# A two-level fast matrix product: a third 7-step inner product, assembly in PSUM banks, and a group ordered by a table

## The chip, the cores and the metric

The kernel runs on one core of a Trainium2 chip. The metric is the device time in microseconds of one execution; of several runs the median is given. Beside it stands one execution taken with the hardware profiler, from which all shares, waits and durations come.

## The reference

```
B, S, D = 8, 2048, 2048            # x: B x S x D float32, w: D x D float32
cs = cumsum(x, axis=1)
diff = cs - (cs shifted by one along axis 1, zero first)
out = matmul(diff, w)              # float32
```

The difference of a running sum is x again, so what is computed is the product of a 16384 x 2048 matrix and a 2048 x 2048 matrix.

## The kernel before

**Tiles.** The rows of x are 128 tiles of 128 rows. The first four (`PLAIN`) are computed directly, in bf16, while w is loaded. The other 124 form 31 groups of four tiles: g, g+1, g+2, g+3. The text calls tile g+2 `h`, g+1 `k` (or "21 of g") and g+3 `l`. A group is a 2 x 2 block matrix: tiles g and h hold the rows of the upper half, k and l those of the lower half, and each tile splits its 2048 columns into two halves (`parts`). w is split into four blocks B11, B12, B21, B22 of 1024 x 1024.

**Seven products.** A group is computed by a scheme with seven products of blocks instead of eight: P1 = A11 B11, P2 = A12 B21, P3 = S4 B22, P4 = A22 T4, P5 = S1 T1, P6 = S2 T2, P7 = S3 T3. The S are sums of blocks of x and made for each group; the T are sums of blocks of w and made once. One product, for the rows of both g and h, is 32 matmuls of 128 x 128 by 128 x 512 if it is done whole (`steps`, L519, and `product`). The same scheme can be put inside a product: then it is seven quarter products of four matmuls (`quarter`, L538, matmuls at L546), 28 in all, and needs four small sums of half rows of x for each group (`sums_in`, L517) and sums of quarter blocks of w (class `Inner`). In the steady groups P2, P3, P4 and P5 are done in that way, P1, P6 and P7 whole: 4 x 28 + 3 x 32 = 208 matmuls. The first group (`group_plain`) does all seven whole, the second (`group` with g = PLAIN + 4) does P2, P3 and P4 by quarters; these two also make the T and the inner sums of w.

**Memory.** The inner sums of w that find no place stand in DRAM (`spill`) and are brought back in each group into one buffer, `flow` (`bring_flow`, L510); other values of that buffer are computed into it by VectorE (`less`, L514, and L850). The sums S1 lie in two tiles of their own, the other S in the place of transposed tiles that are no longer needed.

**Input.** Each tile comes as two f32 halves by DMA (`load`, L100). ScalarE takes its row sums of absolute values (`weigh`, L112), VectorE turns them into a scale (`scale_of`, L129 and L131), and GpSimd into the factor `unit` that the results are multiplied by (L132). ScalarE writes the halves as scaled f16 (`narrow`, L143), and a DMA transposes each half into the tiles that the matmuls read (`turn`, L156).

**Results.** There are eight PSUM banks of 128 x 512 f32. What a bank holds goes to one of seven result tiles c: the first part by ScalarE (`keep`, L554), every further part by VectorE (`add`, L557: c = bank x unit + c). A finished c is stored by DMA (`put`, L568). Before the change each quarter product whose value belongs to two or three results is added to each of them.

**Order.** Every engine gets its instructions in the order in which the program asks for them (`after` chains them on each engine), and all DMAs of the steady part are issued by one queue, SP's. The order inside a group is that of the Python code of `group`. Instructions on different engines wait for each other by semaphores only where they touch the same data or bank.

Of the kernel before, what the change touches and what calls it, by code (L numbers as in the profile page):

```python
# [10 lines left out]
def kernel(  # L11
# [55 lines left out]
    small = ctx.enter_context(tc.tile_pool(name="small", bufs=3))  # L67
    units = ctx.enter_context(tc.tile_pool(name="units", bufs=8))
# [25 lines left out]
    scales = {}  # L94

# [9 lines left out]
    def weigh(t, sides=range(2)):  # L105
        if t < END:
            if t not in sums_of:
                sums_of[t] = small.tile([P, 2], f32, name="m")
            for i in sides:
                after(  # L110
                    "act",
                    lambda: nc.scalar.activation(  # L112
                        waste,
                        where[t][i],
                        ABS,
                        scale=1.0 / ROW,
                        accum_out=sums_of[t][:, i : i + 1],
                    ),
                )

    def scale_of(t):
        if t < END:
            m2 = sums_of.pop(t)
            m = small.tile([P, 1], f32, name="m1")
            s = scales[t] = small.tile([P, 1], f32, name="s")
            u = unit[t] = units.tile([P, 1], f32, name="u")
            after(
                "dve",
                lambda: nc.vector.tensor_scalar(m, m2[:, :1], m2[:, 1:], TINY, ADD, MAX),  # L129
            )  # L130
            after("dve", lambda: nc.vector.reciprocal(s, m))  # L131
            after("pool", lambda: nc.gpsimd.tensor_scalar(u, m, uw, None, MUL))  # L132
# [32 lines left out]
    with ExitStack() as head:  # L165
# [235 lines left out]
        scale_of(PLAIN)  # L401
        for k in range(4, KH):
            block(B11, 0, 0, k, "dve")
# [6 lines left out]
        scale_of(PLAIN + 2)  # L410
        finish_row(1)
# [17 lines left out]
        scale_of(PLAIN + 1)  # L429
        narrow(PLAIN + 1)  # L430
# [52 lines left out]
    class Inner:  # L483
        def __init__(self, b):
            self.Q1, self.Q2 = ([spare.pop() for _ in range(4)] for _ in range(2))
# [15 lines left out]
        def third(self):  # L501
            less(self.t12, self.t22, self.t12)

# [96 lines left out]
    assert not spare  # L600

    def group_plain(g, X, Y, Z, V):
# [27 lines left out]
        scale_of(h + 1)  # L630
        narrow(h + 1)
# [25 lines left out]
        scale_of(g + 4)  # L657
        narrow(g + 4)
# [20 lines left out]
        scale_of(h + 4)  # L679
        less(T4[4:], B21[4:], T2[4:])  # L680
# [10 lines left out]
        scale_of(g + 5)  # L691
        adds(C22h, Y, vh)
# [16 lines left out]
        scale_of(h + 5)  # L709
        C21 = pair()  # L710
        keeps(C21, Y, vh)
        narrow(h + 5)
        less(in_3.Q2, in_3.t22, in_3.Q1)
        turn(h + 5)
# [5 lines left out]
    def group(g, X, Y, q, e, v, w):  # L720
        h = g + 2
        five = g > PLAIN + 4
# [41 lines left out]
        if g == PLAIN + 4:  # L764
            in_3.fourth()
            less(in_4.Q1, in_4.t12, in_4.t11)
        if g > PLAIN + 4:
            total(S1g, A21g, A22g, ADD)
            total(S3g, A11g, A21g, SUB)
            total(S2g, S1g, A11g, SUB)  # L770
# [10 lines left out]
        if g == PLAIN + 4:  # L781
            total(S1g, A21g, A22g, ADD)
        add(C11g[0], q, ug)
        if g == PLAIN + 4:
            total(S3g, A11g, A21g, SUB)
        quarter(e, s1, Q.Q1, True)
        add(C11h[1], e, uh)
        if g == PLAIN + 4:
            total(S2g, S1g, A11g, SUB)
# [10 lines left out]
        if g == PLAIN + 4:  # L800
            total(S2h, S1h, A11h, SUB)
        if g > PLAIN + 4:
            scale_of(next_g)
            narrow(next_g)
            total(S2h, S1h, A11h, SUB)
# [4 lines left out]
        if g == PLAIN + 4:  # L810
            scale_of(next_g)
            narrow(next_g)
        else:
            weigh(next_h)
        load(next_k, 1)
        total(S4g, A12g, S2g, SUB)
        go(P6g, 2)
        C12g = pair()
        keeps(C12g, X, ug)
        if g == PLAIN + 4:  # L820
            weigh(next_h)
# [8 lines left out]
        if five:  # L830
            one()
            two()
        if g > PLAIN + 4:
            scale_of(next_h)
            narrow(next_h)
            load(next_l, 1)
# [9 lines left out]
        if five:  # L846
            one()
            two()
            for k in range(4):
                after('dve', lambda: nc.vector.tensor_tensor(passed[k], in_3.Q4[k], in_3.Q2[k], ADD))  # L850
            a11, a12, a22, s1, s2, s3, s4 = A5
            b11, b12, b22, r1, r2, r3, r4 = A3
            N, R = in_5, in_3
            go(P7g)
            quarter(v, a12, N.t21, True)
            C22g, C22h = [one_c()], []
            keep(C22g[0], v, vg)
            quarter(q, a11, N.t11, True)
            one4()
            add(C22g[0], q, vg)  # L860
            add(C12g[0], q, ug)
            weigh(next_k)
            go(P7g)
            quarter(w, b11, R.t11, True)
            add(C12g[0], w, ug)
            quarter(v, b12, passed, False)
            if g == PLAIN + 8:
                in_5.fourth()
                keep_flow(1)
            else:  # L870
                bring_flow(1)
            add(C12g[0], v, ug)
            put(C12g[0], g, 2)
            turn(next_g, [1])
            go(P7g)
            quarter(e, s1, N.Q1, True)
            C22g += [one_c()]
            C22h = [None, one_c()]
            keep(C22g[1], e, vg)
            keep(C22h[1], e, vh)  # L880
            go(P7g)
            two4()
            scale_of(next_k)
            add(C22g[0], X[0], vg)
            put(C22g[0], g + 1, 2)
            narrow(next_k)
            quarter(q, s2, N.Q2, False)
            add(C22g[1], q, vg)
            add(C12g[1], q, ug)
            quarter(w, r2, R.Q2, False)  # L890
            add(C12g[1], w, ug)
            add(C22g[1], X[1], vg)
            go(P7h)
            quarter(e, r1, R.Q1, False)
            add(C12g[1], e, ug)
            add(C12h[1], e, uh)
            turn(next_k, [0])
            turn(next_h, [0])
            load(next_l, 0)
            go(P7h)  # L900
            quarter(v, s4, N.t22, True)
            add(C22g[1], v, vg)
            put(C22g[1], g + 1, 3)
            load(then, 1)
            quarter(q, s3, N.Q3, False)
            C22h[0] = one_c()
            keep(C22h[0], q, vh)
            add(C22h[1], q, vh)
            add(C12h[1], q, uh)
            go(P7h)  # L910
            quarter(e, a22, passed, True)
            bring_flow(2)
            add(C22h[0], e, vh)
            add(C12h[0], q, uh)
            weigh(next_l)
            quarter(v, r4, R.t22, False)
            add(C12g[1], v, ug)
            put(C12g[1], g, 3)
            go(P7h)
            adds(C22h, Y, vh)  # L920
            puts(C22h, h + 1, 1)
            quarter(e, b22, R.Q4, False)
            add(C12h[0], e, uh)
            quarter(w, r3, R.Q3, False)
            add(C12h[0], w, uh)
            put(C12h[0], h, 2)
            add(C12h[1], w, uh)
            put(C12h[1], h, 3)
            scale_of(next_l)
        else:  # L930
            in_3.third()
            one()
            two()
            scale_of(next_h)
            narrow(next_h)
            load(next_l, 1)
            weigh(next_k)
            seven(A3, in_3, C12g, C12h, P7g)
            turn(next_g, [1])
            turn(next_h, [0])  # L940
            load(next_l, 0)
            scale_of(next_k)
            narrow(next_k)
            in_5.first()
            product((v, w), S1g, T1, True)
            C22g = pair()
            keeps(C22g, (v, w), vg)
            adds(C12g, (v, w), ug)
            puts(C12g, g, 1)
            less(in_4.Q2, in_4.t22, in_4.Q1)  # L950
            product((q, e), S1h, T1, True)
            C22h = pair()
            keeps(C22h, (q, e), vh)
            one4()
            adds(C12h, (q, e), uh)
            puts(C12h, h, 1)
            go(P7g, 2)
            two4()
            turn(next_k, [0])
            adds(C22g, X, vg)  # L960
            puts(C22g, g + 1, 1)
            in_4.fourth()
            keep_flow(2)
            go(P7h, 4)
            adds(C22h, Y, vh)
            puts(C22h, h + 1, 1)
            weigh(next_l)
            scale_of(next_l)
            in_4.third()
            load(then, 1)  # L970
# [32 lines left out]
        if next_g < END:  # L1003
            less(passed, in_2.t21, in_2.Q2)
        turn(next_l, [1])
        if g == PLAIN + 4:
            in_5.third()
# [37 lines left out]
```

## Time and profile before

| | |
|---|---|
| median of three runs | 1485.3 us (1485.26 to 1485.86) |
| profiled execution, span from the first to the last instruction | 1484.2 us |
| median of the runs less that span | 1.1 us |
| TensorE (PE) busy | 1470.2 us, 6795 matmuls |
| VectorE (DVE) busy | 1290.2 us |
| ScalarE (ACT) busy | 914.3 us |
| share of the 16 DMA engines taken by SP's queue | 93.2% |
| granted TensorE clock, mean | 0.999 |
| one steady group | 45.10 us, 208 matmuls |

The page lists for each engine the time in which it had work; matmuls are pipelined, so a busy PE says little on its own. The chain that ended last is followed back from the last instruction, each step to what released it. In the groups, "idle before" is the time the engine had nothing to run ahead of these instructions, and behind the arrow what ended it. A name such as `b` is a PSUM bank, `c` a result tile, `F` the loaded input, `x` the transposed tiles, `inner` and `S` the sums, `W` the blocks of w and the sums made of them.

### The profile page before, as it was taken

How to read it: one execution, taken by the hardware profiler on the slowest of the kernel's cores; microseconds unless marked ns; L12 is line 12 of the kernel's file. 1: busy time of each engine (PE TensorE's matmuls, PEld its weight loads, DVE VectorE, ACT ScalarE, POOL GpSimd, SP SyncE). 2: the span in 40 equal slices, each digit the busy share in tenths (PEclk: the TensorE clock that was granted, in tenths of full speed). 3: DMA queues.
4: the chain of work that ended last, by engine and by line, in shares of the span. 5: the costliest groups of instructions: out<-in, count | busy, mean ns of one | idle time of the engine just before them, and what ended most of it. 6: DMA issues, size and time to landing. Idle time of an engine off the chain costs nothing.

```text
span 1484.2 us, 21118 instructions
## 1 busy us (share of the span) xinstructions
PE 1470.2 (99%) x6795; PEld 663.3 (45%) x6795; DVE 1290.2 (87%) x2434; ACT 914.3 (62%) x1301; POOL 69.5 (5%) x136
## 2 busy tenths in 40 slices
PE   8999999999999999999999999999999999999998
PEld 3444444444444444444444444444444444444443
DVE  7998998888888888888888888888888888888887
ACT  5887566665566665665755666655666656656542
POOL 0110000000000000000000000000000000000000
PEclk9999999999999999999999999999999999999999
DMA  9999989989989999989999998999989999898983
GB/s 359 361 234 295 258 241 267 241 261 272 255 245 262 245 266 268 252 249 250 259 268 264 245 263 238 262 276 253 247 254 250 268 266 253 257 240 260 274 205 128
DMA packets 386255, 382.59 MB, mean 258 GB/s; under 512 B 275744, under 2 KB 275744, under 8 KB 386016
## 3 DMA queue, kind: packets, MB, share of 16 engines
q1 hardware_dynamic: 385584, 379.41, 93.2%
q0 software_dynamic: 560, 1.84, 0.3%
q8 instruction: 53, 0.87, 0.2%
q14 instruction: 58, 0.48, 0.1%
HBM read 180.88 MB, written 135.27 MB: 213 GB/s over the span
## 4 chain that ended last, share of the span: by engine, by line
PE 94%; DMA 2%; DVE 2%; ACT 0%; issue 0%; SPq 0%; DVEq 0%; ACTq 0%
PE b L546 46%; PE b L527 45%; PE b L260 2%; DVE c L557 2%; DMA W<-in_w_dram 2%; DMA W<-in_x_dram 0%; DMA out_dram<-c 0%; ACT wb L244 0%; PE b L385 0%; ACT o L280 0%; ACT c L554 0%; SPq L204 0%; DVEq L1040 0%; DVEq L557 0%; SPq L238 0%
## 5 line engine op out<-in xcount | busy, mean ns | idle before, releaser
L557 DVE SCALAR_TENSOR_TENSOR c<-b,u,c 128x512 f32<-128x512 f32 x1051 | 746.4, 746 | 155.1 <-PE b L546 86.9
L527 PE MATMUL b<-W,x 128*128 128x512 f16 x3072 | 716.4, 379 | 0.0
L554 ACT ACTIVATE c<-b,u 128x512 f32<-128x512 f32 x492 | 314.9, 681 | 335.4 <-PE b L546 170.2
L527 PEld LDWEIGHTS <-x 128*128 128x128 f16 x3072 | 300.6, 98 | 362.5
L143 ACT ACTIVATE F<-F,s 128x1024 f16<-128x1024 f32 x246 | 282.3, 1147 | 111.7 <-DVE s L131 107.6
L112 ACT ACTIVATE waste<-F 128x1024 uint8<-128x1024 f32 x246 | 259.5, 1055 | 95.3 <-DMA F<-in_x_dram 91.2
L546 PEld LDWEIGHTS <-x 128*128 128x128 f16 x1560 | 152.4, 98 | 190.8 <-issue 10.5
L546 PE MATMUL b<-W,x 128*128 128x512 f16 x964 | 232.9, 379 | 1.4
L546 PE MATMUL b<-W,inner 128*128 128x512 f16 x828 | 212.5, 379 | 0.0
L546 PEld LDWEIGHTS <-inner 128*128 128x128 f16 x1068 | 104.5, 98 | 126.0
L546 PE MATMUL b<-W,S 128*128 128x512 f16 x588 | 146.2, 379 | 0.0
L132 POOL TENSOR_SCALAR u<-m,uw 128x1 f32<-128x1 f32 x124 | 64.5, 525 | 1301.1 <-DVE m L129 1293.2
L517 DVE TENSOR_TENSOR x<-x,x 128x1024 f16<-128x1024 f16 (+1 forms) x214 | 120.3, 574 | 5.8 <-PE b L527 0.7
L546 PEld LDWEIGHTS <-S 128*128 128x128 f16 x704 | 68.9, 98 | 83.1
L546 PE MATMUL b<-flow,x 128*128 128x512 f16 x356 | 91.4, 379 | 0.0
L260 PE MATMUL b<-wb,xP 128*128 128x512 bf16 x240 | 57.4, 393 | 5.1 <-ACT wb L244 3.7
L546 PE MATMUL b<-inner 128*128 128x512 f16 x240 | 61.6, 379 | 0.0
L546 PE MATMUL b<-inner,x 128*128 128x512 f16 x240 | 61.6, 379 | 0.0
L112 ACT ACTIVATION_READ_ACCUMULATOR waste<-F 128x1 f32 x246 | 46.6, 189 | 0.0
L517 DVE TENSOR_TENSOR x<-S,x 128x1024 f16<-128x1024 f16 x62 | 42.3, 683 | 3.2
L514 DVE TENSOR_TENSOR flow<-W,inner 128x512 f16<-128x512 f16 x120 | 42.6, 417 | 0.0
L517 DVE TENSOR_TENSOR S<-x,x 128x1024 f16<-128x1024 f16 x62 | 42.2, 681 | 0.0
(65 smaller groups left out, 520.8 us busy)
## 6 DMA issues: line engine op xcount, KB each, us to landing
F<-in_x_dram SPq DMA_DIRECT2D x246, 512.0 KB, 5.3
out_dram<-c SPq DMA_DIRECT2D x492, 256.0 KB, 4.1
flow<-spill SPq DMA_DIRECT2D x57, 512.0 KB, 4.5
W<-in_w_dram SPq DMA_DIRECT2D x32, 512.0 KB, 9.9
W<-in_x_dram SPq DMA_DIRECT2D x16, 256.0 KB, 7.2
x<-F SPq DMA_TRANSPOSE x246, 4.0
out_dram<-o POOLq DMA_DIRECT2D x5, 256.0 KB, 4.1
out_dram<-o SPq DMA_DIRECT2D x5, 256.0 KB, 3.5
```

The costliest lines, as they stand in the source:

```text
L112: lambda: nc.scalar.activation(waste, where[t][i], ABS, scale=1.0 / ROW, accum_out=sums_of[t][:, i : i + 1],),
L132: after("pool", lambda: nc.gpsimd.tensor_scalar(u, m, uw, None, MUL))
L143: lambda: nc.scalar.activation(narrowed(t)[:, ds(i * NH, NH)], where[t][i], COPY, scale=s),
L260: lambda: nc.tensor.matmul(ps[r][n], xP[:, r, ko, :], wb[h, ko][:, ds(n * NB, NB)], start=(ko == 0), stop=(ko == KO - 1),),
L514: after("dve", lambda: nc.vector.tensor_tensor(dst[k], p[k], q[k], SUB))
L517: after("dve", lambda: nc.vector.tensor_tensor(dst.all, p.all, q.all, op))
L527: said = nc.tensor.matmul(to[n], a[k], b[k][:, n, :], start=(first and k == 0), stop=(k == KH - 1), skip_group_check=True,)
L546: said = nc.tensor.matmul(to, a[k], b[k], start=(first and k == 0), stop=(k == 3), skip_group_check=True)
L554: after("act", lambda: nc.scalar.activation(c, p, COPY, scale=u))
L557: after("dve", lambda: nc.vector.scalar_tensor_tensor(c, p, u, c, MUL, ADD))
```

## The change

The second group is now a function of its own (`group_half`), and from the third group on, 29 groups, everything is done by a class `Group`. Its steps have names (`P1.p5` is the quarter product p5 of P1, `P1.s2` a small sum, `P1.fp4` a filling of the flow buffer, `S1.g` a sum of the group, `keep.C11g0`, `add.C12h1.e`, `load0.k`, `turn1.l` and so on), and a table `ORDER` says in what order they are asked for, with -1, 0 or +1 for the group before, this one or the next. Banks and result tiles are taken from the front of a list and put back at its end.

- **P1 by seven quarter products** too, with an `Inner` of B11 (`in_1`): 5 x 28 + 2 x 32 = 204 matmuls in a group.
- **P1 and P5 are assembled in four banks** (`by_seven`): ScalarE copies a bank into another bank (`cg`) and one into a result tile (`ct`), VectorE writes the sum of a bank and that tile into a bank (`m1`, `m2`), and further quarter products accumulate on top. P6 and P7 are accumulated onto the four banks of P1. The results are then read from the finished banks, so a steady group has 27 additions `add` where it had 36, four merges, and five copies by ScalarE.
- **Row sums over the transposes:** S1 is written in the place of A21, S3 over A11, and the four small sums of P4 into the transposed tiles of k and l. The two tiles that held S1 serve as sums of B11.
- **The flow buffer** is filled six times a group: four times by VectorE (P1.p4, P3.p2, P5.p4, P5.p5), twice by DMA (P2.p4, P4.p4).
- The small numbers of a tile (row sums, scale, unit) lie in one tile of a pool of 16, and GpSimd's `unit` is asked for in a step of its own (`unit_of`).
- The last P4 has an order of its own (`END_ORDER`).

The core of the diff:

```diff
+        def by_seven(self, P, h0, h1, g0, g1):
+            self.quarter(P, "p1", h0, True)
+            self.copy(f"{P}.cg", g0, open_banks, h0)
+            self.quarter(P, "p5", h1, True)
+            self.copy(f"{P}.ct", f"{P}t", free, h1)
+            self.quarter(P, "p6", h0, False)
+            self.merge(f"{P}.m1", g1, h0, f"{P}t", fresh=True)
+            self.quarter(P, "p2", g0, False)
+            self.quarter(P, "p7", h0, False)
+            self.merge(f"{P}.m2", h1, h0, f"{P}t", let=True)
+            self.quarter(P, "p3", g1, False)
+            self.quarter(P, "p4", h0, False)
...
+        def copy(self, name, to, pool, b):
...
+                after("act", lambda: nc.scalar.copy(c, p))
...
+        def merge(self, name, to, b, c, fresh=False, let=False):
...
+                after("dve", lambda: nc.vector.tensor_tensor(t, p, s, ADD))
...
+            for a, b in ("gk", "hl"):
+                (A11, A12), (A21, A22) = half[a], half[b]
+                self.step(f"S1.{a}", total, A21, A21, A22, ADD)
+                self.step(f"S2.{a}", total, A11, A21, A11, SUB)
+                self.step(f"S4.{a}", total, A12, A12, A11, SUB)
+                self.step(f"S3.{a}", total, A11, A22, A11, SUB)
...
+    ORDER = """
+    P2.s3+0 keep.C11g0+0 P1.p2+0 load0.g+1 P1.s3+0 keep.C21h0-1 P1.p3+0 P1.p7+0
+    P2.cv+0 S1.g+0 S2.g+0 P2.s4+0 P2.p6+0 P1.m2+0 keep.C11h1+0 add.C21h0.x-1
+    load1.g+1 P1.fp4+0 turn0.l+0 P2.p2+0 P5.p1+0 add.C11h1.e+0 add.C11g0.v+0
+    keep.C11g1+0 P6g.0+0 turn1.l+0 add.C11g1.q+0 S1.h+0 P5.s1+0 put.C12g1-1
+    put.C21h0-1 weigh0.g+1 P1.p4+0 S2.h+0 P2.p3+0 add.C11g1.e+0 P5.cg+0 P2.fp4+0
+    S4.g+0 P2.p7+0 P5.s2+0 weigh1.g+1 load0.h+1 P5.p2+0 scale.g+1 unit.g+1
+    put.C11g0+0 keep.C11h0+0 add.C11h1.q+0 load1.h+1 P6g.2+0 weigh0.h+1 P6h.1+0
+    P6g.1+0 P5.s4+0 P2.p4+0 P5.s3+0 P6g.3+0 keep.C22g0+0 P6h.0+0 P5.fp5+0 S4.h+0
+    P3.s1+0 narrow0.g+1 P5.p5+0 P5.ct+0 put.C21h1-1 put.C11h1+0 keep.C12g0+0
...
+    put.C12h1+0 P1.s1+1 P4.p5+0 keep.C21g1+0 weigh0.l+1 P1.p1+1 P1.cg+1
+    put.C21g0+0 P4.p3+0 P4.p4+0 keep.C21h1+0 add.C21g1.x+0 turn0.k+1
+    add.C21g1.q+0 put.C12h0+0 P2.p1+1 P4.p7+0 P1.s2+1 P1.p5+1 P1.s4+1 weigh1.l+1
+    P1.p6+1 add.C21h1.e+0 P2.s1+1 P1.ct+1 scale.l+1 add.C21h1.q+0 P1.m1+1
+    narrow0.l+1 narrow1.l+1 P2.s2+1 P2.p5+1
+    """
...
+    END_ORDER = """
+    P4.p1 keep.C21g0 P4.p5 keep.C21g1 P4.p6 add.C21g1.q keep.C21h1 P4.p2
+    add.C21g0.x put.C21g0 P4.p3 add.C21h1.e add.C21g1.x put.C21g1 P4.p7
+    add.C21h1.q keep.C21h0 put.C21h1 P4.p4 add.C21h0.x put.C21h0
+    """.split()
```

## The prediction

> **What bounds the kernel now.** I read the page first: busy times, then the chain that ended last.
>
> ```profile
> span 1484.2 us, 21118 instructions
> PE 1470.2 (99%) x6795; PEld 663.3 (45%) x6795; DVE 1290.2 (87%) x2434; ACT 914.3 (62%) x1301; POOL 69.5 (5%) x136
> ...
> q1 hardware_dynamic: 385584, 379.41, 93.2%
> ...
> PE 94%; DMA 2%; DVE 2%; ACT 0%; issue 0%; SPq 0%; DVEq 0%; ACTq 0%
> ```
>
> TensorE works 99% of the span and is 94% of the chain. VectorE (87%) and the DMA engines (93.2%) stand close behind. Next I cut one steady group of four row tiles out of the middle, and the end, by the view of windows (columns: stretch, its length, busy time and count of PE, PEld, DVE, ACT, POOL, granted clock, DMA share, GB/s):
>
> ```profile
> 76.14:124.50 48.36, 48.36 (x225) 21.91 (x224) 46.28 (x95) 39.45 (x56) 5.49 (x6) 1.00 1.02 262
> ...
> 667.00:712.10 45.10, 45.05 (x210) 20.34 (x209) 39.43 (x76) 28.72 (x42) 1.92 (x4) 1.00 0.93 263
> ...
> 1478.70:1484.20 5.50, 0.00 (x0) 0.00 (x0) 1.74 (x3) 0.00 (x0) 0.00 (x0) 0.71 0.38 143
> ```
>
> The first row is the plain group. A steady group takes 45.10 us, and there are 29 of them (29 x 45.10 = 1308 us). In it DVE has 5.7 us to spare. Then the chain of waits over one group boundary (start, length, what):
>
> ```profile
> 1200.09 6.06 PE b L546 x28
> 1206.14 0.03 issue
> 1206.17 0.02 DVEq L557
> 1206.19 0.04 issue
> 1206.24 0.76 DVE c L557
> 1207.00 0.04 issue
> 1207.04 1.02 PE b L546 x4
> 1208.06 6.91 PE b L527 x32
> ```
>
> Thirty-two matmuls take 6.91 us, so a step of four takes 0.864 us, and 52 steps are 44.90 us. The missing 0.20 us is the hop in these lines: a matmul step ends, an addition reads its bank, and the next use of that bank waits. The last matmul's end comes 0.17 us after the pace (a step alone is 1.03 us long), then 0.09 to DVE, 0.76, 0.04 back: 1.06 us. One step between (0.86) covers all but 0.20 of it. This hop is my measure for the new order. It is the only place in a steady group where PE waits. Last, durations by the page's groups (busy time, mean ns) and spacings by the timeline of DVE (start, length):
>
> ```profile
> L557 DVE SCALAR_TENSOR_TENSOR c<-b,u,c 128x512 f32<-128x512 f32 x1051 | 746.4, 746 | 155.1 <-PE b L546 86.9 <-ACT c L554 35.7 <-DVE c L557 0.9
> ...
> L280 ACT COPY o<-b 128x512 f32<-128x512 f32 x10 | 5.2, 599 | 0.0
> ```
>
> ```profile
> 669.11 1.42 DVE L514 TENSOR_TENSOR flow<-W,inner 128x512 f16<-128x512 f16 x4
> ...
> 701.29 6.87 DVE L557 SCALAR_TENSOR_TENSOR c<-b,u,c 128x512 f32<-128x512 f32 x10 [0.83 <-ACT c L554]
> ```
>
> Ten additions in 6.87 us: one starts every 0.68 us though each lasts 0.75. Four f16 subtractions of half a row in 1.42: one every 0.33, each 0.42 long.
>
> **The change, per steady group.** Counts are those of the built programs, divided by 29 groups.
> *Removed on PE:* A11·B11 goes from 32 to 28 matmuls: one step, 0.864 us. 51 steps are 44.04 us. Without any wait that is 45.10 - 44.04 = 1.06 us a group, 30.7 in all, of which 5.8 are the old hop, which the new order no longer has in that place.
> *DVE:* nine additions fewer (P1 and P5 are put together in PSUM and leave as four results each), -9 x 0.68 = -6.1. Four small sums more, 4 x 0.34 = +1.4 (a half-row sum starts every 0.34 too). The fills of the flow buffer go from two to four, eight half rows, 8 x 0.33 = +2.7. Four merges (bank plus f32 tile into a bank), a form without a row: at least 0.33 (the half-row f16 sum), at most 1.5 (two additions); I take 0.68, since the addition has the same bank and f32 operands and width: +2.7. Sum +0.7: 40.1 of 44.04 us, 91%; with the ends of the merge 38.7 and 43.4, below 44.04 either way. By the Trainium skill, page "VectorE: DVE Perf Modes", section on the TRN2 errata, an f32 tensor_tensor of N elements takes (N+151)/0.96 ns, 691 ns here; by that the merge would be 0.06 shorter than the addition's 0.746 and the sum the same within 0.3 us.
> *ACT:* five copies out of banks, three of them into banks (no row; nearest the 599 ns copy out of a bank, the ends being 0.3, half of it, and 0.75): +3.0, 28.7 to 31.7 of 44.04. ACT's idle time hides it; without that cover a copy in the way of PE would cost its 0.6.
> *Moved:* units (0.53 us each) stand alone on POOL, which is busy 1.9 of 45 us; nothing but the results' scaling waits for them. Loads, transposes, results and the two flow loads are the same 34 DMAs on the same SP queue, in another order. S1 now lies over the transposed A21, so the next group's transposes of those tiles wait for P4 and P5.
>
> *Where a stall goes.* I laid the table's DVE steps one behind another at those spacings, none before the matmul step that it reads, with a matmul step every 0.864 us, and looked at what is short. Three hops have no room:
> - P4.p7 writes the bank that add.C21g1.q reads, and that addition stands behind add.C21g1.x, which reads P4.p3, three steps earlier. Three steps are 2.59 us; P4.p3 itself, its end, the hand-over, two additions and the way back are 0.86 + 0.17 + 0.09 + 0.68 + 0.76 + 0.04 = 2.60, plus a hand-over between the two: 0.0 to 0.1 short.
> - P2.p4 reads flow, P5.fp5 fills it anew (1.42), P5.p5 three steps later reads it: 0.86 + 0.26 + 1.42 + 0.04 = 2.58 against 2.59.
> - P5.p1 needs the bank of add.C21h0.x, behind a result that ACT takes behind two row conversions of 1.15: about even as well.
> The merges themselves have room: P1.m1 lies between P1.p6 and P1.p3 with two steps (1.73) against a 1.06 hop. A wait of PE shifts everything behind it and gives the others room, so these do not simply add. With five further places within 0.2 us, and half the old 0.20 as the usual miss of such a balance at each of the three: 0.33 us a group (ends 0 and 0.8). Queued behind a late addition are only DVE's next sums, and behind those the next PE steps.
> *Once:* the first of the 29 groups starts behind the half group's last additions: P1.p1 and P2.p1 (1.73) cover two of these, P1.s1 and s2, about 2.4 us in all: +0.7. The plain group takes four more f16 subtractions (1.3) into 2.1 us of DVE idle, +0.3 at most; later preparations move between the half group and the first steady one and cancel to within 1 us. The end: P4 alone, keep.C21g0 short by 0.1, but one addition at the end where two stood. Together +1.0 (0 to 2).
>
> **Sum.** Group 44.04 + 0.33 = 44.37; saved 0.73 x 29 = 21.2; span 1484.2 - 21.2 + 1.0 = 1464.0. The median of the runs, 1485.3, lies 1.1 above this span: 1465.
>
> **Rivals.**
> *DVE sets the pace.* Merges or fills a tenth longer than I took, in several of the tight hops, and PE's wait is 0.7 a group: 0.36 x 29 = 10.4 saved, 1476. For it: 91% and the hops above. Against: before, at 87%, one hop of 0.20 was all. 0.20.
> *Transposes land late: slower.* Tile l's second row half is converted at the group's start (two conversions, 2.3 us after scale.l), then turn0.l issues (1.3), turn1.l lands 4.0 later, and S1.h reads it about 8.7 us after scale.l: 0.8 us of room. Behind S1.h stand seven DVE steps without a gap up to add.C11h1.q, for which P2.p4 waits, so lateness beyond 0.8 goes to PE. Landing takes 3.1 to 7.8 us in the trace (median 4.0). From a mean of 4.0 + 0.8 + 1.06 = 5.9 us on the gain is gone; at 6.5 it is 1.7 a group, (1.7 - 1.06) x 29 = +19: 1505. For it: the DMA engines go from 93% to 93 x 45.1 / 44.4 = 95% of the time, and SP's queue is in order. Against: DVE's sums waited for a transpose once in the whole span, 1.3 us. 0.14.
> *The clock falls.* PE pauses briefly more often; at half clock (0.50 is granted in the last 2.2 us, where PE stands still) four steps a group cost 4 x 0.86 = 3.5 us more: (3.5 - 0.73) x 29 = +80, 1565. Against: 1.00 in all groups with the 0.20 us pause. 0.02. The Trainium skill names the mechanism ("TensorE: Matmul & The Clock Gate", section on psum-queue depth-cycling: short pauses between groups of matmuls, going round the banks, make the clock oscillate); by that rule the change would be a loss. The trace so far doesn't show it.
> *The change does not remove the matmuls:* excluded, the built program holds 116 fewer.
>
> **How the numbers follow.** Forecast 0.62 (waits of 0 to 0.5: 1455 to 1471), DVE's pace 0.20 (1471 to 1483), late transposes 0.14, clock 0.02, unnamed 0.02. The range 1455 to 1483 holds the first two. No change means within 0.2%, 3 us, about what a measurement of this kernel can tell. Faster: 0.62 + 0.18 + 0.01 = 0.81. Same: 0.02 + 0.01 = 0.03. Slower: 0.12 + 0.02 + 0.02 = 0.16.
>
> **What would show it.** Right: group period between 44.1 and 44.6, PE x6679, DVE near 40 us a group, the merge near 0.7 us, PE's waits all on DVE or ACT in the named hops. Wrong: waits of PE or of DVE's sums on transposes (late landing), DVE over 43 us a group, a clock under 1.00 in mid-run, or a period at or above 45.1.

## The result and the profile after

The changed kernel takes 1499.95 us (median of four runs, 1498.14 to 1505.42) where the kernel before takes 1485.58 on the same chip: a ratio of 1.0102 [1.0085, 1.012], 1% slower. The forecast was 1465 us. The profiled execution is the longest of the four, 1505.42 us with a span of 1503.6; sums made in its trace stand some 5.5 us above the median.

The same lines of the page as before:

```profile
span 1503.6 us, 20817 instructions
PE 1456.9 (97%) x6679; PEld 652.7 (43%) x6679; DVE 1284.5 (85%) x2645; ACT 973.5 (65%) x1446; POOL 60.5 (4%) x136
...
q1 hardware_dynamic: 385728, 379.93, 90.2%
...
PE 67%; DMA 17%; DVE 11%; ACT 3%; issue 2%; SPq 1%; DVEq 0%; ACTq 0%
```

The 116 matmuls are gone, and PE, DVE and the queue q1 are all less busy as a share of the span; but the chain has changed hands: PE fell from 94% of it to 67%, DMA rose from 2% to 17% and DVE from 2% to 11%. A steady group in the view of windows, and then the durations that the forecast had no row for, from the page's groups:

```profile
667.10:712.78 45.68, 44.64 (x206) 19.95 (x204) 39.09 (x83) 29.72 (x45) 1.59 (x4) 1.00 0.96 250
```

```profile
L1021 DVE TENSOR_TENSOR b<-b,c 128x512 f32<-128x512 f32 x116 | 80.0, 690 | 2.5 <-PE b L561 2.4
L1014 ACT COPY b<-b 128x512 f32<-128x512 f32 x87 | 50.1, 575 | 24.4 <-PE b L561 13.1
```

DVE has 39 us of work in a group and ACT 30, both less than forecast; the merge takes 0.690 us and a copy from bank to bank 0.575. The group takes 45.68 us all the same. From here on "period" is the spacing of the first merges of successive groups, the mean of 28: here 45.76, uneven, 44.18 to 48.81. Who waits for whom (total, times, longest):

```profile
ACT c L569 <- DMA out_dram<-c: 100.0, 98, 4.0
...
DVE x L532 <- DMA x<-F: 37.4, 28, 3.2
...
PE b L542 <- ACT c L569: 15.5, 13, 2.9
PE b L561 <- DVE c L572: 14.9, 30, 1.5
```

PE's waits sum to 40 us, against 6 before. DVE's row sums (L532) wait for a transpose in nearly every group, 1.34 us a time; before, they did so once. 22 of these 28 waits, 31.5 us, are those of S1.h for turn1.l. ACT waits for stores of results (L569), 100 us against 5.7. The chain of waits shows the first of these on its way to PE:

```profile
679.38 3.16 DMA F<-in_x_dram
682.54 6.63 DMA x<-F
689.26 0.70 DVE x L532
689.98 0.42 DVE inner L532
...
691.67 0.60 DVE x L532
...
692.84 0.74 DVE c L572
...
693.63 1.02 PE b L561 x4
```

A load, then turn1.l, which lands 6.63 us after its issue; S1.h at 689.26 and behind it, without a gap, the sums and additions up to the one at 692.84; and PE's next step of four matmuls as soon as that is done. It is the path of the forecast's second rival, step for step. What stood ahead of the transposes is told by the timeline of SP's queue (start, length of issuing, what). The kernel before, around the last transpose of tile l:

```profile
655.81 0.38 SPq L100 DMA_DIRECT2D F<-in_x_dram  x1
...
665.82 3.01 SPq L156 DMA_TRANSPOSE x<-F  x2
668.92 0.55 SPq L568 DMA_DIRECT2D out_dram<-c  x1
669.56 0.39 SPq L100 DMA_DIRECT2D F<-in_x_dram  x1
670.05 0.92 SPq L568 DMA_DIRECT2D out_dram<-c  x2
671.06 1.85 SPq L156 DMA_TRANSPOSE x<-F  x1
673.00 3.68 SPq L100 DMA_DIRECT2D F<-in_x_dram  x3
```

The changed kernel, around turn0.l and turn1.l:

```profile
678.33 0.95 SPq L583 DMA_DIRECT2D out_dram<-c  x1
679.38 1.73 SPq L100 DMA_DIRECT2D F<-in_x_dram  x2
681.21 5.92 SPq L160 DMA_TRANSPOSE x<-F  x2
```

Before, load1.g goes out 15 us ahead of turn1.l (655.81), behind load0.l; turn0.l is the second of the pair at 665.82; load0.g (669.56) and two results stand between it and turn1.l; the three loads behind are those of tiles h and k. In the new table load0.g and load1.g go out right ahead of both transposes. The two issues then take 5.92 us instead of about 3, turn1.l's alone 4.59.

In the kernel before turn1.l landed late as well, 6.1 us after its issue (mean of 24 groups, 5.3 to 7.8), but the sum that reads it, S1 of tile h, did not start until 6.8 to 8.2 us after that issue, so nothing waited. In the group shown, 7.7 us after it:

```profile
678.79 0.68 DVE L517 TENSOR_TENSOR S<-x,x 128x1024 f16<-128x1024 f16 x1
```

In the changed kernel turn1.l lands 6.9 us after its issue (mean of 22 groups, 5.6 to 8.6), and S1.h is asked for earlier.

### The profile page after: what moved, and what is told of

Same layout as the page of the kernel before. It is cut to its first block, busy times and chain, and to the rows that moved or that the text cites. A ratio compares the mean times of both kernels' runs of the same rounds, so it can differ in the third digit from the quotient of the medians.

```text
span 1503.6 us, 20817 instructions
## 1 busy us (share of the span) xinstructions
PE 1456.9 (97%) x6679; PEld 652.7 (43%) x6679; DVE 1284.5 (85%) x2645; ACT 973.5 (65%) x1446; POOL 60.5 (4%) x136
## 3 DMA queue, kind: packets, MB, share of 16 engines
q1 hardware_dynamic: 385728, 379.93, 90.2%
## 4 chain that ended last, share of the span: by engine, by line
PE 67%; DMA 17%; DVE 11%; ACT 3%; issue 2%; SPq 1%; DVEq 0%; ACTq 0%
PE b L561 38%; PE b L542 26%; DMA x<-F 10%; DVE c L572 4%; DMA out_dram<-c 4%; DVE x L532 3%; PE b L264 2%; DVE inner L532 2%; DMA W<-in_w_dram 2%; DMA F<-in_x_dram 1%; ACT c L569 1%; DVE b L1021 1%; ACT F L147 1%; SPq L160 1%; DMA W<-in_x_dram 0%
## 5 line engine op out<-in xcount | busy, mean ns | idle before, releaser
L572 DVE SCALAR_TENSOR_TENSOR c<-b,of,c 128x512 f32<-128x512 f32 x790 | 564.2, 744 | 114.7 <-ACT c L569 70.6
L542 PE MATMUL b<-W,x 128*128 128x512 f16 x2144 | 509.3, 381 | 20.0 <-ACT c L569 15.5
L569 ACT ACTIVATE c<-b,of 128x512 f32<-128x512 f32 x492 | 321.7, 683 | 276.2 <-PE b L561 137.3
L147 ACT ACTIVATE F<-F,of 128x1024 f16<-128x1024 f32 x246 | 282.0, 1146 | 53.8 <-DVE of L130 51.5
L532 DVE TENSOR_TENSOR x<-x,x 128x1024 f16<-128x1024 f16 (+1 forms) x388 | 221.4, 583 | 43.9 <-DMA x<-F 37.4
L561 PEld LDWEIGHTS <-inner 128*128 128x128 f16 x1648 | 161.2, 98 | 195.3 <-DVE inner L532 1.7
L561 PE MATMUL b<-flow,x 128*128 128x512 f16 x588 | 151.7, 380 | 4.1 <-DVE c L572 4.0
L561 PE MATMUL b<-inner 128*128 128x512 f16 x472 | 121.1, 379 | 0.0
L136 POOL TENSOR_SCALAR of<-of,uw 128x1 f32<-128x1 f32 x124 | 55.6, 459 | 1337.2 <-DVE of L128 1329.2
L928 DVE TENSOR_TENSOR flow<-W 128x512 f16<-128x512 f16 x232 | 82.8, 418 | 6.0 <-PE b L561 5.8
L1021 DVE TENSOR_TENSOR b<-b,c 128x512 f32<-128x512 f32 x116 | 80.0, 690 | 2.5 <-PE b L561 2.4
L1014 ACT COPY b<-b 128x512 f32<-128x512 f32 x87 | 50.1, 575 | 24.4 <-PE b L561 13.1
L1014 ACT COPY c<-b 128x512 f32<-128x512 f32 x58 | 33.6, 580 | 37.5 <-PE b L561 37.4
L532 DVE TENSOR_TENSOR inner<-x 128x512 f16<-128x512 f16 x117 | 49.3, 422 | 7.6 <-DMA x<-F 5.2
L532 DVE TENSOR_TENSOR inner<-x,inner 128x512 f16<-128x512 f16 x117 | 49.2, 421 | 4.0
L532 DVE TENSOR_TENSOR inner<-inner,x 128x512 f16<-128x512 f16 x117 | 48.4, 413 | 0.1
```

The lines of the kernel that those rows point to most:

```text
L147: lambda: nc.scalar.activation(narrowed(t)[:, ds(i * NH, NH)], where[t][i], COPY, scale=s),
L532: after("dve", lambda: nc.vector.tensor_tensor(dst.all, p.all, q.all, op))
L542: said = nc.tensor.matmul(to[n], a[k], b[k][:, n, :], start=(first and k == 0), stop=(k == KH - 1), skip_group_check=True,)
L561: said = nc.tensor.matmul(to, a[k], b[k], start=(first and k == 0), stop=(k == 3), skip_group_check=True)
L569: after("act", lambda: nc.scalar.activation(c, p, COPY, scale=u))
L572: after("dve", lambda: nc.vector.scalar_tensor_tensor(c, p, u, c, MUL, ADD))
```

## The experiments

Three causes were possible. **Late transposes:** tile l's pair lands late because it stands behind two loads of 512 KB, and DVE's sums carry that to PE. **Result tiles:** ACT waits for stores before its `keep`, and PE for ACT. **No room on the engines:** the hops of the forecast (additions, fills, merges) are tight whatever the DMA does.

**The loads behind the transposes**

```diff
-P1.p2+0 load0.g+1 P1.s3+0 ...  load1.g+1 P1.fp4+0 turn0.l+0 ... turn1.l+0 add.C11g1.q+0
+P1.p2+0 P1.s3+0 ...            P1.fp4+0 turn0.l+0 ... turn1.l+0 load0.g+1 load1.g+1 add.C11g1.q+0
```

> Only the table is edited: the two loads of the next group's tile g are issued behind the two transposes of tile l, not ahead of them. Theory T (the transposes of l sit behind two 512 KB loads in the queue, land 6.5 to 7 us after their issue, and S1.h, then add.C11h1.q, then P2.p4 wait): they land in 3.5 to 4.5 us, the 37 us in which DVE waits for transposes fall under 10, and the time falls by 10 us or more, to 1480 to 1490, less what the later loads cost ACT's weigh0.g (its place in the table is not changed). Rival R (too few result tiles: ACT waits 100 us for stores and holds banks): that wait stays near 100 us and the time moves by under 5 us, 1495 to 1505. Rival P (the hops between PE and DVE are too tight by themselves): same, 1495 to 1505.

Measured: 1515.09 us (1514.07 to 1517.83), 1.0202 [1.0187, 1.0217] of the kernel before: slower still, where 1480 to 1490 were expected; period 46.07. But the wait that it aimed at is gone, and another has come:

```profile
ACT waste L112 <- DMA F<-in_x_dram: 164.8, 60, 5.2
...
PE b L561 <- ACT b L1014: 28.8, 25, 2.3
...
DVE x L532 <- DMA x<-F: 3.8, 5, 1.3
```

DVE's wait for transposes fell from 37.4 to 3.8 us. The loads, however, are now late for weigh0.g, and the copy P5.cg stands behind that on ACT. A swap of two evils, which decides nothing on the size of the first.

**Nine result tiles instead of seven.** The two tiles that held S1 serve as result tiles; the sum `in_1.Q2` is left out, and P1.p6 reads the sum of T1 in its place.

```diff
-    in_1 = Inner(B11, (in_5.Q1, [t.all[:, n, :] for t in reversed(S1) for n in range(2)]))
+    in_1 = Inner(B11, (in_5.Q1, in_5.Q2))
...
+    free.extend(t.all.rearrange("p a n -> p (a n)").bitcast(f32) for t in S1)
```

> Nine result tiles where there are seven: from the third group on the two tiles that hold sums of B11 are result tiles too. Left out: P1.p6 uses the sums of T1 instead of its own, so these values are not those of the reference; the work per group is the same. Rival R (result tiles): ACT's wait for stores falls from 100 us to under 15, and the time by 10 us or more, to 1475 to 1490. Theory T (transposes behind loads): ACT's wait falls too, but the time only by 0 to 6 us, since DVE still waits for the transposes of l. Rival P: no change, 1495 to 1505.

Measured: 1496.8 us (1494.15 to 1502.55), 1.0081 [1.0058, 1.0104], period 45.66. ACT's wait for stores is gone, DVE's for transposes is 42.8 us. Within the scatter the time is that of the changed kernel: the 100 us that ACT waited cost at most some 3 us.

**Both together**

> Both edits at once (with the same values left out as with nine tiles). If transposes and result tiles are the whole loss, the group period falls to 44.1 to 44.5 us and the time to 1460 to 1470, as was forecast for waits of 0.3 us a group; if the hops between PE and DVE are too tight (rival P) it stays above 1480 with neither transposes nor stores in the waits.

Measured: 1504.46 us (1501.63 to 1510.45), 1.0135 [1.0109, 1.0162], period 45.73: the first edit's new wait (weigh0.g on its load, PE behind ACT's copies 25.5 us) remains.

**A quarter of each store.** Every `put` stores 128 of its 512 columns; the rest of the output is left unwritten.

```diff
-nc.sync.dma_start(out2[ds(t * P, P), ds(at * NB, NB)], c)
+nc.sync.dma_start(out2[ds(t * P, P), ds(at * NB, 128)], c[:, :128])
```

> Left out: three quarters of every stored result tile in the groups (128 of 512 columns are stored), which takes nearly 1 MB of the 4.25 MB... of each tile's DMA traffic away and changes nothing else. Theory T with R (DMA lateness of any kind): transposes land in 3 to 4 us, ACT's wait for stores disappears, period 44.1 to 44.6, time 1457 to 1472. Rival P (hops): the period stays near 45.5 and the time above 1490.

Measured: 1470.41 us (1470.25 to 1470.58), 0.9898 [0.9878, 0.9918]. The steady part in the view of windows (the last three columns are the clock, the DMA share and GB/s):

```profile
306.20:1351.20 1045.00, 1038.44 (x4790) 467.74 (x4789) 917.60 (x1932) 698.39 (x1060) 37.16 (x93) 1.00 0.73 190
```

97.5 of the 379.9 MB that the queue moved are gone. With the DMA engines busy 73% of that time instead of 92% in the changed kernel, the period is 44.54 us, and 13 of 28 groups take 44.10 to 44.15. All instructions of PE, DVE and ACT are there, in the same order. So the engines have the room that the forecast gave them (44.37), and the loss lies with the transfers. One part of what was expected did not come: tile l's transposes still stand behind two loads and land after 6.2 us, not 3 to 4. They are issued a little earlier, and land on the mean 8.4 us after the group's first merge instead of 9.4; DVE's wait of x for transposes falls to 12.7 us.

**DVE's sums later.** S1.h, S2.h, P5.s1 and P5.s2 behind add.C11h1.q, P6h.1 behind P6g.3, so that a late transpose finds no addition behind it that PE needs soon.

```diff
-turn1.l+0 add.C11g1.q+0 S1.h+0 P5.s1+0 put.C12g1-1 ... P1.p4+0 S2.h+0 P2.p3+0 ... P2.p7+0 P5.s2+0 weigh1.g+1
-... add.C11h1.q+0 load1.h+1 ...
+turn1.l+0 add.C11g1.q+0 put.C12g1-1 ... P1.p4+0 P2.p3+0 ... P2.p7+0 weigh1.g+1
+... add.C11h1.q+0 S1.h+0 S2.h+0 P5.s1+0 P5.s2+0 load1.h+1 ...
```

> Only the table is edited, all values are as in the reference: S1.h, S2.h, P5.s1 and P5.s2 stand behind add.C11h1.q in DVE's order, and the two first steps of P6h behind P6g.3, so that S1.h is due about 2.8 us later (3.6 us of room for the transposes of tile l instead of 0.8) and nothing that PE needs soon stands behind it. Theory T (late transposes of l, handed to PE by the steps behind S1.h): PE's waits for DVE at P2.p4 go, and the period falls by 0.6 to 1.2 us from 45.76, to 1465 to 1482. If result tiles (R) are the larger part: ACT's wait for stores stays at 80 to 100 us and the time falls by under 8 us, 1492 or more. If DMA lateness simply moves on to the next place (W: loads, stores and transposes are late everywhere, since the same bytes must pass in an order with little room): 1485 to 1497, with DVE's wait for transposes under 15 us and the waits for loads or stores higher.

Measured: 1488.4 us (1486.12 to 1495.74), 1.0028 [1.0015, 1.0041]; period 45.03, DVE's wait of x for transposes 4.1 us. 11.5 of the lost microseconds are back with every transfer left in its place. The rest did not come back: the time lies in the range that was expected if lateness moves on to the next place, and PE now waits 10.6 us for transfers into the flow buffer, for which it did not wait in the changed kernel.

**The same with nine result tiles** (`in_1.Q2` left out as above)

> The same table with nine result tiles (P1.p6 again with the sums of T1: its values are not the reference's). T and R together: ACT's wait for stores under 15 us, DVE's for transposes under 15 us, period 44.3 to 44.8, 1462 to 1476. W: 1480 or more.

Measured: 1484.2 us (1480.62 to 1486.62), 0.9989 [0.9979, 0.9998], period 45.09. At most a few microseconds lie with the result tiles; 1462 to 1476 were expected if these and the late transposes were the whole loss.

**The sums later, and one load half a group earlier**

```diff
-    load1.g+1 P1.fp4+0 turn0.l+0
+    P1.fp4+0 turn0.l+0
...
-load0.l+1 P5.p4+0
+load0.l+1 load1.g+2 P5.p4+0
```

> The same table as the first, and load1.g issued nearly half a group earlier, behind load0.l, so that only one load stands ahead of the transposes of l; values as in the reference. T: these transposes land in 4 to 5 us instead of 6.6 to 7.1; the time is 2 to 10 us below that of the first. W: the load now delays the transposes of h and k instead, the same time within 4 us or more.

Measured: **1480.68 us** (1480.37 to 1480.84), 0.9968 [0.9955, 0.9981], period 44.82: faster than both kernels. Tile l's pair, behind one load, lands after 5.7 us (4 to 5 were expected). The other half of what was expected shows as well: DVE's wait of `inner` for the other transposes rises from 6.8 to 27.4 us.

**One load earlier, and nothing else.** The diff is the one just shown, on the changed kernel.

> The changed kernel with its sums as they were, and one load issued half a group earlier (load1.g of the group after next, behind load0.l). The transposes of tile l then stand behind one load instead of two. If the loss is that landing: VectorE's wait of x for transposes falls from 37 us to under 15 and the time to 1482 to 1490. If the loss is VectorE's order of sums, which the step before also changed, the time stays within 0.3% of the changed kernel, 1496 to 1504.

Measured: 1482.53 us (1480.41 to 1483.76), 0.9976 [0.9965, 0.9987], period 44.95. One name moved in the table brings 17.4 us, and the sums stand where they stood. The new place, behind load0.l, is the one that load1.g had in the kernel before. Its queue, around tile l's pair, and its waits:

```profile
670.99 1.11 SPq L100 DMA_DIRECT2D F<-in_x_dram  x1
672.20 4.54 SPq L160 DMA_TRANSPOSE x<-F  x2
```

```profile
DVE inner L532 <- DMA x<-F: 33.1, 52, 2.6
PE b L561 <- DVE c L572: 16.1, 24, 1.9
DVE x L532 <- DMA x<-F: 9.6, 10, 1.6
```

PE's waits for ACT's `keep` (L569), 15.5 us in the changed kernel, have gone too, although ACT's own wait for stores grew to 162.9: they came with the late sums. (With nine result tiles they went as well, but PE then waited 12.4 us for the late sums themselves.)

DVE's waits for transposes add up to the same as in the changed kernel: 33.1 + 9.6 = 42.7 us here, 5.2 + 37.4 = 42.6 there. What fell is the wait of x, and what rose is that of `inner`, the small sums: turn0.h now stands behind the moved load as well as load0.l, a flow load and a result, and lands after 4.35 us instead of 3.4, and 28 of the 52 waits, 22.1 us, are for it (3 waits, 1.9 us, in the changed kernel). So the move is a swap too, of a dear wait for a cheap one.

**No load ahead of the pair.** As the last, and load0.g behind turn1.l, weigh1.g before weigh0.g, scale.g and unit.g behind P5.s4.

```diff
-P1.p2+0 load0.g+1 P1.s3+0 ... turn1.l+0 add.C11g1.q+0 ... weigh0.g+1 P1.p4+0 ... weigh1.g+1 load0.h+1
+P1.p2+0 P1.s3+0 ... turn1.l+0 load0.g+1 add.C11g1.q+0 ... weigh1.g+1 P1.p4+0 ... weigh0.g+1 load0.h+1
```

> The changed kernel, its sums as they were, with no load ahead of tile l's transposes: load1.g half a group earlier (as in the run with one load ahead), load0.g behind turn1.l; weigh1.g now before weigh0.g, and scale.g moved behind P5.s4, so that the later load0.g holds nothing. If landing behind loads is what costs: the pair lands in 3.5 to 4 us instead of 5.5, VectorE's wait of x falls under 6 us, and the time comes to 1470 to 1479. If the remaining loss is the wait of inner for the other transposes (33 us) or the results' stores, the time stays at 1480 to 1484; if load0.g now holds ScalarE, PE waits on ScalarE and it is 1485 to 1500.

Measured: 1483.64 us (1482.69 to 1485.29), 0.9988 [0.9979, 0.9998]. The pair lands in 3.5 us as expected, and it brings nothing more; DVE's other wait (inner, 32.0 us) is much that of the run before (33.1).

**The same with the sums later**

> The same with S1.h, S2.h, P5.s1 and P5.s2 behind add.C11h1.q as well. If the late sums only guard against late transposes, they bring nothing more once these are early: within 0.2% of the run before this one. If transposes are still late now and then: 2 to 5 us less than it.

Measured: 1482.77 us (1480.7 to 1486.93), 0.9984 [0.9975, 0.9994], the same: once the transposes are early, the order of the sums is worth nothing that can be told.

**Two tries at what was left**, on the 1480.68 us version. First S1.g and S2.g behind P1.m2 and add.C21h0.x:

> The version with the late sums and the load ahead (1480.7 us), and S1.g and S2.g moved behind P1.m2 and add.C21h0.x, so that a late transpose of tile k no longer holds the addition whose bank P5.p1 needs. If the rest of the loss is that hop at the group's start, PE's waits on DVE fall from 13.4 us to under 6 and the time to 1471 to 1476 (period 44.5 to 44.6). If the rest lies with the sums P1.s1 and the additions behind them at the group's end, it stays at 1479 to 1482.

Measured: 1501.77 us (1501.22 to 1502.22), 1.0109 [1.0093, 1.0124], period 45.55. P5.p1 reads S1.g, and now waits for it in almost every group:

```profile
PE b L561 <- DVE c L572: 17.0, 44, 1.6
PE b L561 <- DVE x L532: 8.2, 28, 0.3
```

Where they stood, the two sums filled time in which DVE had nothing else ready: in the new order its small sums wait for PE 18.2 us and its merges 13.1 (0.4 before the move).

Second, turn1.h of the next group in the place of turn1.k and the other way round, on top of it. P3.p4 stands between the two places and reads S4.h, which lies where turn1.h writes; so in this kernel P3.p4 reads the next group's tile.

> As the run before this one, and turn1.h of the next group issued in the place of turn1.k and the other way round, so that the half rows which P1.s1 reads land one issue (1.3 us) earlier. If P1.s1 holds the additions at the group's end: VectorE's wait of inner for transposes falls from 27 us to under 12 and the time by a further 2 to 6 us, to 1468 to 1474. If what arrives later in exchange (turn1.k, read by S1.g) matters as much: no gain or up to 5 us slower.

Measured: 1660.95 us (1660.5 to 1665.19), 1.1187 [1.117, 1.1203]. PE waits for that transfer itself, 114.4 us. The run tells nothing on P1.s1: as long as S4.h lies there, turn1.h can't go ahead of P3.p4.

**What a load ahead costs a transpose.** From the SP timelines of these runs (300 to 1360 us) I took the pairs of transposes that were issued back to back, and some single ones, sorted by the loads right ahead of them, with the mean of their (for a pair, median) landings:

| kernel | loads ahead | number | issue of both, us | landing, us |
|---|---|---|---|---|
| before | 0 | 48 | 2.9 | 3.8 |
| before (turn1.g and turn1.h, single) | 0 | 46 | - | 4.0 |
| before (turn0.g, single) | 1 | 24 | - | 5.2 |
| before (turn1.l, single) | 1, then two results | 24 | - | 6.1 |
| changed | 0 | 50 | 3.0 | 3.5 |
| changed | 2 | 20 | 5.9 | 7.1 |
| one load earlier | 1 | 15 | 4.4 | 5.5 |
| no load ahead of the pair | 0 | 72 | 2.9 | 3.5 |

About 1.8 us a load in the pairs, and 1.2 to 2.1 for the single ones. At the 258 GB/s of the steady part (version with one load earlier) 512 KB take 2.0 us, so it is as if the load's bytes went through first; that is worked out, not shown. The Trainium skill ("DMA: Bandwidth & Descriptors", section "Queues, rings and completion order") says that each DMA engine takes the descriptors of one ring in order; by that rule a transpose can't start before the loads issued ahead of it on the same queue have started. The table agrees, with 3.5, 5.5 and 7.1 us.

## Why the prediction was wrong

- **The step that failed** is "Loads, transposes, results and the two flow loads are the same 34 DMAs on the same SP queue, in another order", costed at nothing, together with the landing of 4.0 us taken for turn1.l. The other order is the loss: load1.g moved from behind load0.l, 15 us ahead, and load0.g from between tile l's transposes, to right ahead of both; S1.h is due 8.7 - 2.3 - 1.3 = 5.1 us after turn1.l's issue by the forecast's own figures, and turn1.l lands after 6.9. Moving load1.g back brings back 17.4 us (1499.95 to 1482.53), and asking for the sums later, with every transfer in its place, 11.5.
- **The rival "Transposes land late"** named the path and nearly the price: 1.7 us a group and 1505 at a mean landing of 6.5. The group's excess over 44.04 is 1.72 (45.76), the time 1499.95, the profiled execution 1505.42. Its landing was mis-sized: 4.0 is the median over all transposes, but turn1.l itself, with a load and two results right ahead, took 6.1 in the very same trace, and by the rival's own formula the gain is gone from 5.9 on. So the rows on record before the change already spoke for it. Its chance of 0.14 came from the 4.0, and from the reason against it, "DVE's sums waited for a transpose once in the whole span": before, S1 of tile h started 6.8 to 8.2 us after that issue, and the change asks for it earlier. That the price fits so well is in part luck: the room was larger than the 0.8 us worked out (its terms, 8.7 - 2.3 - 1.3 - 4.0, leave 1.1; an estimate from the run is 6.9 - 4.0 - 1.1 = 1.8, where 1.1 is the 31.5 us by 29 groups), and PE's waits for ACT and the clock, below, are not in it.
- **The sum itself** was right where transfers leave it alone. PE x6679; merge 0.690 for 0.68; DVE 39.1 us a group for 40.1, ACT 29.7 for 31.7. By the formula of the Trainium skill ("VectorE: DVE Perf Modes", section on the TRN2 errata) the merge was estimated at 691 ns; the trace agrees, with 690. With a quarter of the stores, period 44.54 for 44.37 and a span of 1468.5: 1464.0 + 29 x 0.17 is 1468.9, so the one-off term holds too. That 44.54 lies so near 44.37 is in part luck: in the 13 groups of 44.10 to 44.15 all waits together cost 0.06 to 0.11 us, so the hops were taken too dear at 0.33, and in the others DVE still waits for transposes (12.7 us in all).
- **DVE's pace** and the three tight hops are not the cause: the quarter stores leave them all in place. The reason given for more DMA pressure (93% to 95%) was wrong in sign, 90.2%, since the kernel got longer.
- **The clock** fell only as a consequence. Three stretches below 0.995 lie in the steady part, each behind a wait of PE over 2 us (2.06, 2.45 and 2.87). One of them in the view of windows (behind the length come the busy times of PE, PEld, DVE, ACT and POOL; the third number from the end is the clock):

```profile
369.00:370.00 1.00, 0.00 (x0) 0.03 (x1) 1.00 (x2) 0.66 (x1) 0.00 (x0) 1.00 1.08 389
370.00:371.00 1.00, 0.92 (x4) 0.39 (x4) 0.97 (x5) 0.03 (x1) 0.23 (x1) 0.93 1.03 307
371.00:372.00 1.00, 1.00 (x4) 0.44 (x3) 1.00 (x3) 0.00 (x0) 0.05 (x1) 0.50 0.93 295
```

PE waited 2.06 us up to 370.08, and for some 3.4 us behind it the clock stands at 0.50 (by microsecond 0.93, 0.50, 0.50, 0.50, 0.86): 1.7 us lost. Three of these are 5 us of the profiled execution. A fourth wait, of 2.10 us up to 1060.6, left the clock alone. What tells them apart can be worked out from the traces. The low stretches are 3.413 us long and begin a whole multiple of 3.413 us apart (here 228.7 and 232.1 us, 67 and 68 times; in the run with turn1.h in the place of turn1.k 15 times, over and over). Cut each of the 14 traces into such stretches, counted from a start of half clock (in a trace without one in mid-run, the one at its end): while the groups run, PE stood still for 2.01 us or more in each of the 34 stretches that half clock followed, and for 1.93 us or less in every other. The wait of 2.10 us lies across two, with 1.89 us in the first. In the version with one load earlier PE's longest wait in a steady group is 1.9 us and the mean clock 1.000; the short pauses round the banks that the forecast weighed did nothing.

**What stays open.** The best versions stand at 1481 to 1484 us, some 16 to 19 above the forecast. In the version with one load earlier 0.58 us a group (44.95 against 44.37) are left, and PE waits for additions that stand behind DVE's sums of tiles g, h and k, which wait for their transposes (33.1 us for those of h, 9.6 for others). `inner` waits 27.4 to 33.1 us in the five kernels that have load1.g behind load0.l and keep turn1.k in its place, and 2.6 to 8.0 in the seven, the changed one among them, that have it elsewhere; what that wait is worth by itself no run shows. With a quarter of the stores 0.17 are left; whether an order of the table exists that does it at full traffic, the two tries above didn't show.

## What to carry to other kernels

A new order of the same transfers can cost more than the work that it saves: in an in-order queue, write down for each transfer that something waits for what stands right ahead of it and how long after its issue it is read, before and after, and take its landing from its own rows in the trace or from rows with the same neighbours, not from the median of all. That nothing waited for it before says only that it was read late enough. Where a wait is removed and the time doesn't follow, look at what was moved to remove it: the loads behind the transposes cured one wait and made another that cost more; one load moved half a group ahead made one that cost less. To tell "the engines have no room" from "the data come late", cut the traffic and leave the instructions: one run with quarter stores did it.

## What was not expected of the hardware

- Issuing a transpose behind two loads held SP's queue 4.59 us (4.4 on the mean of 22 groups), where one alone takes 1.24 to 1.4; everything queued behind it went out only then.
- Whether a wait of PE of some 2 us brings 3.4 us of half clock depended on where it fell: 2.06 us did and 2.10 us did not. By stretches of 3.413 us on a fixed grid, 2.01 us of standing still in one of them was enough in these traces and 1.93 us was not.
- The total of an engine's waiting says little. ACT's 100 us for stores were worth some 3 us at most, and DVE's 42.6 us for transposes stayed 42.7 while the time fell by 17 us: what counted was which sums waited, and what stood behind them.
